# Five channel tiles of an up projection by seven products of summed quarters

## The chip, the cores and the metric

The kernel runs on one core of one Trainium2 chip. The metric is the time of one execution in device microseconds (us); a lower number is better. TensorE (PE) multiplies, VectorE (DVE), ScalarE (ACT) and GpSimd (POOL) do the elementwise work, and SyncE (SP) issues most of the loads.

## What is computed

The reference is one decoder layer over 512 positions and 1024 channels. The change lies in its last part, the gated MLP:

```python
h = rmsnorm(x, norm_ffn_pre[l])
u = causal_depthwise_conv(h @ w_ffn_up[l], ffn_conv_w[l], ffn_conv_b[l])
u_gate, u_val = jnp.split(u, 2, axis=-1)
y = (jax.nn.gelu(u_gate, approximate=True) * u_val) @ w_ffn_down[l]
x = x + rmsnorm(y, norm_ffn_post[l])
```

`h` is 512 x 1024 and `w_ffn_up` is 1024 x 5632: 2816 gate channels and 2816 value channels. The convolution looks back over two positions in each channel. Everything is float32.

## The kernel before

A float32 product is made of three matmuls in the format fp32r: each operand is split into a high part (an ACT copy that rounds) and a low part (a DVE subtraction, both in `split`, L81 to L88), and `mm3` (L127 to L130) adds high by high, high by low and low by high.

The up projection works channel-major. One channel tile is 128 gate channels and the 128 value channels that belong to them; there are 22 tiles, `f` from 0 to 21. Product `i = 2f` is the gate half of tile `f` and `i = 2f + 1` the value half. Each product has the weights as the stationary operand (128 x 128 blocks, eight of them over the 1024 input channels) and the normalized input `h1h`, `h1l` (high and low, transposed, both in tiles named hT) as the moving one, 512 positions at a time: 8 x 3 = 24 matmuls of 512 columns into one PSUM bank (`up_products`, L792 to L803). The first four products (`EARLY`) run in two halves of 256 columns (L764 and L802), because the second half of the input comes later.

The weights of a product are one 512 KB load into a `raw` buffer (four of them), issued on SP by `issue` (L95 to L117), and a split into a `whi` and a `wlo` buffer (three of each). `unit(b_up[i])` issues two products ahead.

The bank of a product goes through `conv` (L805 to L811): an ACT pass with the last tap and the bias, and two DVE passes that add the other two taps from the bank. The gate half takes a GELU on ACT (L822). The loop (L813 to L833) then multiplies the two halves on POOL into `gpair` (L829), and behind every fourth tile of the first twenty POOL makes four sums for the down projection (`sums`, L783 to L790). That projection already runs as seven products of summed quarters per 512 hidden channels.

PE runs in the order of the program, and POOL does so from L850 on. ACT and DVE are ordered by the planner at build time: among the instructions that are ready in its own model of time, the one that stands first in the program. On the chip each engine then goes through its list in that fixed order.

Of the kernel before, what the change touches and what calls it, by code (L numbers as in the profile page):

```python
# [26 lines left out]
NF = FH // P  # L27
# [11 lines left out]
def tile_hybrid_layer(  # L39
# [8 lines left out]
    act, dve, pool, pe, sp = nc.scalar, nc.vector, nc.gpsimd, nc.tensor, nc.sync  # L48
# [5 lines left out]
    wp = ctx.enter_context(tc.tile_pool(name="wp", bufs=3))  # L54
    mp = ctx.enter_context(tc.tile_pool(name="mp", bufs=2))
# [4 lines left out]
    ap = ap_stack.enter_context(tc.tile_pool(name="ap", bufs=2))  # L60
# [627 lines left out]
    h1l = T(mp, [P, KD, SEQ], F32R, "hT", 2)  # L688
    h1h = T(mp, [P, KD, SEQ], F32R, "hT", 2)
# [47 lines left out]
    banks = [[PT(tg) for tg in tags] for tags in ("ss", "tt")]  # L737
# [33 lines left out]
    fp = ctx.enter_context(tc.tile_pool(name="fp", bufs=2))  # L771
    c_tile = lambda: T(fp, [P, 512], F32, "c", 4)
    c_next = [c_tile()]
    gpair = [T(fp, [P, 4, 2, 256], F32, "G", NG) for _ in range(NG)]
    gsum = [[t[:, i, :] for i in range(3)] for t in (T(fp, [P, 3, 512], F32, "S", NG - 1) for _ in range(NG - 1))]
    gsum.append([T(mp, [P, 512], F32, "o", 3)[:] for _ in range(3)])
    grest = T(fp, [P, NF - NS, SEQ], F32, "gN", 1)

    def quarters(d):

        return [[gpair[d][:, 2 * c + r].rearrange("p j c -> p (j c)") for r in range(2)] for c in range(2)]

    def sums(d):  # L783

        (a11, a12), (a21, a22) = quarters(d)
        s1, s2, s4 = gsum[d]
        pool.tensor_tensor(s1, a21, a22, op=ALU.subtract)
        pool.tensor_tensor(s2, s1, a11, op=ALU.subtract)
        pool.tensor_tensor(a21, a11, a21, op=ALU.subtract)
        pool.tensor_tensor(s4, a12, s2, op=ALU.add)  # L790

    def up_products(i):  # L792

        if i in early:
# [18 lines left out]
    for f in range(NF):  # L813
# [7 lines left out]
        cg = conv(2 * f, banks[0])  # L821
        act.activation(cg[:], cg[:], AF.Gelu_apprx_tanh)  # L822
        if f:
            banks.append(list(up_products(2 * f + 1))[-1])
            issue(b_up[min(2 * f + 3, 2 * NF - 1)])
        cv = conv(2 * f + 1, banks[1])
        if f < NS:
            halves2 = lambda ap: ap.rearrange("p (c n) -> p c n", c=2)
            pool.tensor_tensor(gpair[f // 4][:, f % 2 :: 2, f % 4 // 2, :], halves2(cg[:]), halves2(cv[:]), op=ALU.mult)  # L829
        else:  # L830
            pool.tensor_tensor(grest[:, f - NS, :], cg[:], cv[:], op=ALU.mult)
        if f < NS and f % 4 == 3:
            sums(f // 4)  # L833
# [16 lines left out]
    ctx.enter_context(tc.manual_schedule(engines={mybir.EngineType.Pool}))  # L850
# [28 lines left out]
    def prepare(i):  # L879
# [76 lines left out]
    for i, (n, d) in enumerate(seq):  # L956
# [78 lines left out]
```

## Time and profile before

| | us |
|---|---|
| median of three runs | 828.42 (828.24 to 828.62) |
| the profiled execution | 828.08 |
| its span | 826.0 |
| PE busy | 812.1 |
| DVE busy | 496.5 |
| ACT busy | 399.3 |
| POOL busy | 138.5 |

The profiled execution is 2.08 us longer than its span. The granted clock of TensorE over the span is 0.997 of full speed. Busy times of PE overlap from one matmul to the next, so a pitch (start to start) is read for a matmul and not its duration.

### The profile page before, as it was taken

What the parts mean: (1) busy time and instruction counts of PE and PEld (TensorE: products, weight loads), DVE (VectorE), ACT (ScalarE), POOL (GpSimd) and SP (SyncE); (2) the same over time, 40 slices, a digit from 0 to 9 for tenths busy, and PEclk for the clock granted to TensorE, in tenths of its full rate; (3) what the DMA queues carried; (4) which work ended last, traced back from release to release, by engine and by line L of the source; (5) the groups of instructions that cost most, each with busy time, mean ns of one, the idle gap of its engine ahead of it and who ended that gap; (6) DMA issues with size and microseconds to landing.
All of it is one profiled execution on the core that took longest, in us unless ns stands there. A gap on an engine that the chain in (4) does not pass through costs nothing.

```text
span 826.0 us, 10558 instructions
## 1 busy us (share of the span) xinstructions
PE 812.1 (98%) x3955; PEld 683.8 (83%) x3955; DVE 496.5 (60%) x825; ACT 399.3 (48%) x693; POOL 138.5 (17%) x117
## 2 busy tenths in 40 slices
PE   6999999999999999999999999999999999999996
PEld 6888888888888888888888898888888888888885
DVE  5846576667667665634564555444554445678775
ACT  6735555556656655432352444343343333567552
POOL 5000000000001010112213101414131413442301
PEclk9999999999999999999999999999999999999998
DMA  9732223323332233324354203333333333696922
GB/s 298 232 94 79 74 84 90 87 85 103 88 92 78 82 102 90 101 85 127 115 183 137 77 27 112 92 102 102 101 87 93 102 102 102 153 222 162 223 83 102
DMA packets 123121, 93.99 MB, mean 114 GB/s; under 512 B 3543, under 2 KB 107167, under 8 KB 123071
## 3 DMA queue, kind: packets, MB, share of 16 engines
q1 hardware_dynamic: 116287, 79.16, 32.1%
q0 software_dynamic: 6160, 13.11, 8.1%
q10 hardware_dynamic: 624, 1.06, 0.3%
q8 instruction: 31, 0.51, 0.2%
q14 instruction: 19, 0.16, 0.1%
HBM read 91.18 MB, written 2.14 MB: 113 GB/s over the span
## 4 chain that ended last, share of the span: by engine, by line
PE 96%; DMA 2%; SPq 1%; issue 1%; DVE 0%; ACT 0%; DVEq 0%; POOLq 0%; POOL 0%
PE pj L128 22%; PE pj L129 22%; PE pj L130 22%; PE t L461 2%; PE s L486 2%; PE s L923 2%; PE s L922 2%; PE s L924 2%; PE t L923 1%; PE t L922 1%; PE t L924 1%; PE o L470 1%; PE o L469 1%; PE o L923 1%; PE o L922 1%; PE o L924 1%
## 5 line engine op out<-in xcount | busy, mean ns | idle before, releaser
L128 PE MATMUL pj<-hT,whi 128*128 128x512 f32 (+1 forms) x704 | 273.8, 389 | 0.0
L129 PE MATMUL pj<-hT,whi 128*128 128x512 f32 (+1 forms) x704 | 271.0, 385 | 0.0
L130 PE MATMUL pj<-hT,wlo 128*128 128x512 f32 (+1 forms) x704 | 271.0, 385 | 0.0
L85 DVE TENSOR_TENSOR wlo<-raw,whi 128x1024 fp32r<-128x1024 f32 x127 | 164.2, 1294 | 176.4 <-ACT whi L84 176.3
L84 ACT ACTIVATE whi<-raw 128x1024 fp32r<-128x1024 f32 x131 | 138.5, 1058 | 172.5 <-PE pj L129 131.4
L130 PEld LDWEIGHTS pj<-hT,wlo 128*128 128x128 f32 x704 | 132.3, 188 | 26.5
L128 PEld LDWEIGHTS pj<-hT,whi 128*128 128x128 f32 x704 | 132.4, 188 | 24.5
L129 PEld LDWEIGHTS pj<-hT,whi 128*128 128x128 f32 x704 | 132.5, 188 | 24.2
L602 POOL TENSOR_TENSOR mx<-mx,gt 128x512 f32<-128x512 f32 x16 | 23.0, 1436 | 379.2 <-DVE gt L601 379.2
L829 POOL TENSOR_TENSOR G<-c,c 128x512 f32<-128x512 f32 x20 | 25.8, 1288 | 167.2 <-DVE c L810 149.4
L128 PE MATMUL pj<-oT,whi 128*128 128x512 f32 (+1 forms) x128 | 48.1, 376 | 0.0
L129 PE MATMUL pj<-oT,whi 128*128 128x512 f32 (+1 forms) x128 | 47.0, 367 | 0.0
L130 PE MATMUL pj<-oT,wlo 128*128 128x512 f32 (+1 forms) x128 | 46.9, 367 | 0.0
L84 ACT ACTIVATE pt<-t 128x512 fp32r<-128x512 f32 (+2 forms) x48 | 24.3, 543 | 36.9 <-PE t L461 36.8
L85 DVE TENSOR_TENSOR pt<-t,pt 128x512 fp32r<-128x512 f32 (+2 forms) x48 | 28.5, 621 | 20.0 <-ACT pt L84 19.5
L488 ACT ACTIVATE P<-P,tiny 128x256 f32<-128x256 f32 (+1 forms) x64 | 33.0, 517 | 14.0 <-DVE tiny L487 13.8
L822 ACT ACTIVATE c<-c 128x512 f32<-128x512 f32 x22 | 13.9, 632 | 42.9 <-DVE c L810 42.9
L810 DVE SCALAR_TENSOR_TENSOR c<-pj,convw,c 128x510 f32<-128x510 f32 x40 | 30.0, 750 | 1.4
L808 ACT ACTIVATE c<-pj,convw 128x512 f32<-128x512 f32 x40 | 30.4, 760 | 0.0
L809 DVE SCALAR_TENSOR_TENSOR c<-pj,convw,c 128x511 f32<-128x511 f32 x40 | 29.7, 743 | 0.0
L130 PEld LDWEIGHTS pj<-oT,wlo 128*128 128x128 f32 x128 | 24.6, 192 | 3.8
L128 PEld LDWEIGHTS pj<-oT,whi 128*128 128x128 f32 x128 | 24.6, 192 | 3.3
(346 smaller groups left out, 1284.6 us busy)
## 6 DMA issues: line engine op xcount, KB each, us to landing
raw<-in_w_in_dram SPq DMA_DIRECT2D x46, 512.0 KB, 3.9
raw<-in_w_ffn_up_dram SPq DMA_DIRECT2D x44, 512.0 KB, 3.9
hT<-in_w_ffn_down_dram POOLq DMA_DIRECT2D x13, 512.0 KB, 8.3
raw<-in_w_ffn_down_dram POOLq DMA_DIRECT2D x12, 512.0 KB, 8.2
raw<-in_w_mem_kv_dram SPq DMA_DIRECT2D x8, 512.0 KB, 5.9
raw<-in_w_out_dram SPq DMA_DIRECT2D x8, 512.0 KB, 3.3
raw<-in_w_ffn_down_dram SPq DMA_DIRECT2D x8, 512.0 KB, 3.4
mx<-in_x_dram SPq DMA_DIRECT2D x12, 256.0 KB, 4.9
```

The source lines that it names most:

```text
L84: act.activation(hi, src, AF.Copy)
L85: eng.tensor_tensor(lo, src, hi.bitcast(F32), op=ALU.subtract)
L128: pe.matmul(ps, wh, xh, start=start, stop=False)
L129: pe.matmul(ps, wh, xl, start=False, stop=False)
L130: pe.matmul(ps, wl, xh, start=False, stop=stop)
L488: act.activation(dst, dst, AF.Exp, bias=mn[:, i : i + 1], scale=-1.0, accum_out=sm[:, i : i + 1])
L808: act.activation(c[:], ps[:], AF.Identity, scale=convw[:, 88 + ch : 89 + ch], bias=convw[:, 132 + ch : 133 + ch])
L809: dve.scalar_tensor_tensor(c[:, 1:512], ps[:, 0:511], convw[:, 44 + ch : 45 + ch], c[:, 1:512], op0=ALU.mult, op1=ALU.add)
L810: dve.scalar_tensor_tensor(c[:, 2:512], ps[:, 0:510], convw[:, ch : ch + 1], c[:, 2:512], op0=ALU.mult, op1=ALU.add)
L922: pe.matmul(ps[:], xh, wh, start=st, stop=False, skip_group_check=True)
L923: pe.matmul(ps[:], xh, wl, start=False, stop=False, skip_group_check=True)
L924: pe.matmul(ps[:], xl, wh, start=False, stop=end, skip_group_check=True)
```

## The change

Tiles 6, 8, 10, 12 and 14 (`SUP`) are computed in another way; tiles 7, 9, 11, 13 and 15 are computed as before, but their matmuls are interleaved with those of the tile ahead of them (`tile_pair`). All other tiles keep the loop.

For a tile in `SUP` the weights [gate | value] and the input are cut into quarters: input channels 0 to 511 and 512 to 1023, gate and value, positions 0 to 255 and 256 to 511. Seven products (`seventh`) of 4 x 3 = 12 matmuls of 256 columns each, of sums of weight quarters with sums of input quarters, replace the 48 matmuls of 512 columns. Three banks collect them; partial results are copied to SBUF or combined there (`p1_`, `u2_`, `p5_`, `row_g`, `row_v`), and `conv` reads the rows of SBUF in place of a bank.

Per tile in `SUP`, DVE makes four sums of weight quarters (`weight_sums`, 128 x 512 each), and there are splits of two whole weight tiles, of one half tile, and of the summed gate weights (`late`). The sums of the input are made once, by `input_sums`: eight POOL instructions over 128 x 1024 elements and eight splits of 128 x 512, one step of it behind each of tiles 0 to 4. They and `late` lie in buffers that tiles 0 to 15 don't need yet: four of the five `gpair` buffers, one of the `gsum` buffers, and buffers of the down projection. The order of POOL is that of the program from ahead of the loop on.

```diff
+SUP = (6, 8, 10, 12, 14)
...
     for i in range(2, 2 * NF):
-        up_block(i)
+        if i // 2 not in SUP:
+            up_block(i)
...
-    gpair = [T(fp, [P, 4, 2, 256], F32, "G", NG) for _ in range(NG)]
...
+    big_tile = lambda dt=F32: T(fp, [P, 2048], dt, "G", NG)[:]
...
+    parts = [big_tile().rearrange("p (a k c) -> p a k c", a=2, k=4) for _ in range(3)]
+    late = big_tile(F32R)
...
+        def whole(q, dst):
+            k, c = quarter_in[q]
+            pool.tensor_tensor(dst, h1h[:, k, c].bitcast(F32), h1l[:, k, c].bitcast(F32), op=ALU.add)
...
+        whole(3, a21)
+        yield
+        whole(4, a22)
+        pool.tensor_tensor(s1, a21, a22, op=ALU.subtract)
+        parted(1, s1)
+        yield
+        whole(1, a11)
+        pool.tensor_tensor(s2, s1, a11, op=ALU.subtract)
+        parted(2, s2)
+        yield
+        pool.tensor_tensor(a11, a11, a21, op=ALU.subtract)
+        parted(3, a11)
+        yield
+        whole(2, a12)
+        pool.tensor_tensor(a12, a12, s2, op=ALU.add)
+        parted(4, a12)
...
+    def weight_sums(raws):
+
+        (g0, g1), (v0, v1) = ((r[:, 0:512], r[:, 512:1024]) for r in raws)
+        first = wpair()
+        split(*first, raws[0])
+        split(*b22[0], v1)
+        for dst, other in ((g0, v0), (v0, v1), (v1, g0), (g1, v1)):
+            dve.tensor_tensor(dst, dst, other, op=ALU.add)
+        return first
...
+    def tile_pair(f, raws, first):
...
+        w_v = wpair()
+        split(*w_v, raws[1])
+        split(late_h, late_l, raws[0])
+        by, bx = PT("t"), PT("s")
+        seventh(by, first, 0, quarter_of(0, 0), True)
+        act.activation(p1_, by[:, 0:256], AF.Copy)
+        seventh(bx, first, 1, quarter_of(4, 0), True)
+        dve.tensor_tensor(row_g[:, 0:256], bx[:, 0:256], p1_, op=ALU.add)
+        steps(ng, 4)
+        seventh(by, w_v, 1, sum_of(2), False)
+        act.activation(u2_, by[:, 0:256], AF.Copy)
+        issue(b_up[2 * f + 3])
+        bz = PT("s")
+        seventh(bz, (late_h, late_l), 0, sum_of(1), True)
+        act.activation(p5_, bz[:, 0:256], AF.Copy)
+        cg_n = gate(2 * f + 2, steps(ng, 4))
+        raws = fetch_up(f + 2) if more else None
+        seventh(by, w_v, 0, sum_of(3), False)
+        dve.tensor_tensor(row_v[:, 256:512], p5_, by[:, 0:256], op=ALU.subtract)
+        first = weight_sums(raws) if more else None
+        issue(b_up[2 * f + (6 if more else 4)])
+        steps(nv, 4)
+        seventh(bz, w_22, 0, sum_of(4), False)
+        dve.tensor_tensor(row_v[:, 0:256], bz[:, 0:256], u2_, op=ALU.subtract)
+        cv = conv(2 * f + 1, row_v)
+        seventh(by, (late_h, late_l), 1, quarter_of(4, 256), False)
+        act.activation(row_g[:, 256:512], by[:, 0:256], AF.Copy)
+        gated(f, gate(2 * f, row_g), cv)
+        gated(f + 1, cg_n, conv(2 * f + 3, steps(nv, 4)))
+        return raws, first
+
+    ctx.enter_context(tc.manual_schedule(engines={mybir.EngineType.Pool}))
...
+        gated(f, cg, conv(2 * f + 1, banks[1]))
+        if f < SUP[0]:
+            next(making)
```

## Rows read from the trace of the kernel before

**Rows 1.** Parts 1 and 4 of the page: the busy time of each engine with its share of the span and its instructions, and the shares of the chain that ended last.

```profile
PE 812.1 (98%) x3955; PEld 683.8 (83%) x3955; DVE 496.5 (60%) x825; ACT 399.3 (48%) x693; POOL 138.5 (17%) x117
...
PE 96%; DMA 2%; SPq 1%; issue 1%; DVE 0%; ACT 0%; DVEq 0%; POOLq 0%; POOL 0%
```

**Rows 2.** Stretches of 20 us of the up projection: length, then busy time of PE, PEld, DVE, ACT and POOL with the instructions, the granted clock, the DMA share and GB/s; the last line sums ten such stretches.

```profile
545.00:565.00 20.00, 20.00 (x90) 16.57 (x89) 11.15 (x13) 8.12 (x11) 1.63 (x2) 1.00 0.30 89
...
sum 200.00, PE 200.00 PEld 169.03 DVE 100.16 ACT 77.19 POOL 46.58; mean PE 20.00 PEld 16.90 DVE 10.02 ACT 7.72 POOL 4.66
```

**Rows 3.** PE in order of time where the loop goes over from halves of 256 columns to products of 512 columns: start, duration, engine, line, operation, out<-in, shape.

```profile
495.35 0.28 PE L130 MATMUL pj<-hT,wlo 128*128 128x256 f32 x1
495.47 0.40 PE L128 MATMUL t<-hT,whi 128*128 128x512 f32 x1
...
496.86 0.39 PE L128 MATMUL t<-hT,whi 128*128 128x512 f32 x1
```

**Rows 4.** ACT, DVE and POOL in order of time over two products of the loop; the bracket is the idle time of the engine before the instruction and what ended it.

```profile
544.43 1.06 ACT L84 ACTIVATE whi<-raw 128x1024 fp32r<-128x1024 f32 x1 [3.71 <-PE pj L129]
545.39 0.76 ACT L808 ACTIVATE c<-pj,convw 128x512 f32<-128x512 f32 x1
545.52 1.23 DVE L85 TENSOR_TENSOR wlo<-raw,whi 128x1024 fp32r<-128x1024 f32 x1 [2.77 <-ACT whi L84]
546.66 0.74 DVE L809 SCALAR_TENSOR_TENSOR c<-pj,convw,c 128x511 f32<-128x511 f32 x1
...
549.87 1.06 ACT L84 ACTIVATE whi<-raw 128x1024 fp32r<-128x1024 f32 x1 [0.95 <-PE pj L129]
...
555.31 1.06 ACT L84 ACTIVATE whi<-raw 128x1024 fp32r<-128x1024 f32 x1 [3.71 <-PE pj L129]
```

**Rows 5.** PE in order of time in the early halves: the first and the last of 25 matmuls of 256 columns in a row.

```profile
476.45 0.28 PE L128 MATMUL pj<-hT,whi 128*128 128x256 f32 x1
...
479.33 0.28 PE L128 MATMUL pj<-hT,whi 128*128 128x256 f32 x1
```

**Rows 6.** PE in order of time at the end of six matmuls of 256 columns that stand between matmuls of 512.

```profile
70.53 0.28 PE L557 MATMUL s<-r,r 128*128 128x256 f32 x1
...
71.25 0.40 PE L128 MATMUL pj<-hT,whi 128*128 128x512 f32 x1
...
72.64 0.39 PE L128 MATMUL pj<-hT,whi 128*128 128x512 f32 x1
```

**Rows 7.** DVE's groups by form from 505 to 685 us: busy time, mean ns of one, idle time before.

```profile
L85 DVE TENSOR_TENSOR wlo<-raw,whi 128x1024 fp32r<-128x1024 f32 x33 | 40.5, 1226 | 89.6 <-ACT whi L84 89.6
L810 DVE SCALAR_TENSOR_TENSOR c<-pj,convw,c 128x510 f32<-128x510 f32 x32 | 24.0, 750 | 1.1
L809 DVE SCALAR_TENSOR_TENSOR c<-pj,convw,c 128x511 f32<-128x511 f32 x32 | 23.8, 743 | 0.0
L85 DVE TENSOR_TENSOR xl<-G,xh 128x512 fp32r<-128x512 f32 x3 | 2.1, 684 | 0.0
```

**Rows 8.** ACT's groups by form from 470 to 685 us, columns as above.

```profile
L84 ACT ACTIVATE whi<-raw 128x1024 fp32r<-128x1024 f32 x36 | 38.2, 1061 | 77.4 <-PE pj L129 72.8 <-PE t L129 3.3 <-issue 1.3
L808 ACT ACTIVATE c<-pj,convw 128x512 f32<-128x512 f32 x34 | 25.8, 760 | 0.0
L822 ACT ACTIVATE c<-c 128x512 f32<-128x512 f32 x19 | 12.0, 632 | 36.5 <-DVE c L810 36.5
L87 ACT ACTIVATE hT<-t,gam 128x256 fp32r<-128x256 f32 x5 | 2.4, 475 | 6.8 <-PE t L266 6.7
L84 ACT ACTIVATE xh<-G 128x512 fp32r<-128x512 f32 x3 | 1.8, 613 | 0.0
```

**Rows 9.** All instructions of L85, the low half of a split: count, then shortest, median and longest duration in ns, first and last start.

```profile
L85 DVE TENSOR_TENSOR r<-s,r x10: 416/424/425, 86.2 to 324.8; 128x256 fp32r<-128x256 f32 x10
...
L85 POOL TENSOR_TENSOR wlo<-raw,whi x4: 2347/2387/2412, 5.5 to 460.0; 128x1024 fp32r<-128x1024 f32 x4
```

**Rows 10.** POOL in order of time from the product of tile 3 on.

```profile
521.14 1.29 POOL L829 TENSOR_TENSOR G<-c,c 128x512 f32<-128x512 f32 x1 [9.59 <-DVE c L810]
522.50 1.29 POOL L787 TENSOR_TENSOR S<-G 128x512 f32<-128x512 f32 x1
523.88 2.26 POOL L788 TENSOR_TENSOR S<-S,G 128x512 f32<-128x512 f32 x1
526.09 1.30 POOL L789 TENSOR_TENSOR G<-G 128x512 f32<-128x512 f32 x1
527.35 1.29 POOL L790 TENSOR_TENSOR S<-G,S 128x512 f32<-128x512 f32 x1
532.01 1.29 POOL L829 TENSOR_TENSOR G<-c,c 128x512 f32<-128x512 f32 x1 [3.37 <-DVE c L810]
542.90 1.28 POOL L829 TENSOR_TENSOR G<-c,c 128x512 f32<-128x512 f32 x1 [9.60 <-DVE c L810]
```

**Rows 11.** DVE in order of time beside the third of these POOL instructions.

```profile
523.76 1.23 DVE L85 TENSOR_TENSOR wlo<-raw,whi 128x1024 fp32r<-128x1024 f32 x1 [2.77 <-ACT whi L84]
```

**Rows 12.** DVE in order of time near 717 us.

```profile
717.40 2.25 DVE L85 TENSOR_TENSOR wlo<-raw,whi 128x1024 fp32r<-128x1024 f32 x1
```

**Rows 13.** POOL in order of time at the same place.

```profile
716.99 1.59 POOL L831 TENSOR_TENSOR gN<-c,c 128x512 f32<-128x512 f32 x1
```

**Rows 14.** Part 6 of the page, the loads of the up weights: line, engine, operation, count, KB each, median us from issue to landing.

```profile
raw<-in_w_ffn_up_dram SPq DMA_DIRECT2D x44, 512.0 KB, 3.9
```

More of the change, by code (lines that the diff above doesn't have):

```diff
@@ new lines, in tile_hybrid_layer, with input_sums, parted @@
+    late = big_tile(F32R)
+    late_h, late_l = late[:, 0:1024], late[:, 1024:2048]
+    rows_s = T(fp, [P, 3, 512], F32, "S", NG - 1)
+    row_g, row_v = rows_s[:, 0, :], rows_s[:, 1, :]
+    p1_, u2_ = rows_s[:, 2, 0:256], rows_s[:, 2, 256:512]
+    p5_ = T(fp, [P, 512], F32, "gffn", 2)[:, 0:256]
+    b22 = T(fp, [P, 1024], F32R, "gN", 1)
+    b22 = [(b22[:, 0:512], b22[:, 512:1024])]
+    hsum = {}
+    def input_sums():
+        low, high = slice(0, 256), slice(256, 512)
+        quarter_in = {1: (slice(0, 4), low), 2: (slice(4, 8), low), 3: (slice(0, 4), high), 4: (slice(4, 8), high)}
+        a11, a21 = parts[0][:, 0], parts[0][:, 1]
+        a12, a22 = parts[1][:, 0], parts[1][:, 1]
+        s1, s2 = parts[2][:, 0], parts[2][:, 1]
+        def whole(q, dst):
+            k, c = quarter_in[q]
+            pool.tensor_tensor(dst, h1h[:, k, c].bitcast(F32), h1l[:, k, c].bitcast(F32), op=ALU.add)
+        def parted(j, src):
+            hsum[j] = []
+            for q in range(2):
+                hi, lo = (homes.pop(0).rearrange("p (k c) -> p k c", k=2) for _ in range(2))
+                split(hi, lo, src[:, 2 * q : 2 * q + 2, :])
+                hsum[j].append((hi, lo))
+        homes = [T(fp, [P, 512], F32R, tag, 3)[:] for tag in ("xh", "xl") for _ in range(3)]
+        homes += [T(mp, [P, 512], F32R, tag, n)[:] for tag, n in (("op", 2), ("gt", 2), ("o", 3)) for _ in range(n)]
+        for _ in range(2):
+            t = T(mp, [P, 1280], F32R, "P", 2)
+            homes += [t[:, 0:512], t[:, 512:1024]]
+        whole(3, a21)
[14 more added lines that the diff above has]
+        parted(4, a12)
+        b22.append((homes.pop(0), T(fp, [P, 512], F32R, "gffn", 2)[:]))
+        yield
+        yield
@@ L797, in up_products @@
         else:
-            u = unit(b_up[i])
-            ps = PT("t" if i < EARLY + 2 else "pj")
+            if i < 2 * SUP[0]:
+                issue(min(b_up[i] + 2, b_up[2 * SUP[0] - 1]))
+            u = units[b_up[i]] if i < 2 * max(SUP) + 4 else unit(b_up[i])
+            ps = PT("t" if i < EARLY + 2 else "s" if i < EARLY + 4 else "pj")
             a = 0
@@ L805, in conv @@
     def conv(i, ps):
+        ps = ps[:]
         ch = i // 2 + NF * (i % 2)
@@ L811, in conv, with gated @@
         return c
-    for f in range(NF):
+    def gated(f, cg, cv):
+        if f < NS:
+            if f % 4 == 0:
+                gpair[f // 4] = T(fp, [P, 4, 2, 256], F32, "G", NG)
+            halves2 = lambda ap: ap.rearrange("p (c n) -> p c n", c=2)
+            pool.tensor_tensor(gpair[f // 4][:, f % 2 :: 2, f % 4 // 2, :], halves2(cg[:]), halves2(cv[:]), op=ALU.mult)
+        else:
+            pool.tensor_tensor(grest[:, f - NS, :], cg[:], cv[:], op=ALU.mult)
+        if f < NS and f % 4 == 3:
+            d = f // 4
+            if d < NG - 1:
+                t = T(fp, [P, 3, 512], F32, "S", NG - 1)
+                gsum[d] = [t[:, i, :] for i in range(3)]
+            else:
+                gsum[d] = [T(mp, [P, 512], F32, "o", 3)[:] for _ in range(3)]
+            sums(d)
@@ new lines, in gate, with steps, fetch_up @@
+    def gate(i, bank):
+        cg = conv(i, bank)
+        act.activation(cg[:], cg[:], AF.Gelu_apprx_tanh)
+        return cg
+    def steps(gen, n):
+        for _ in range(n):
+            ps = next(gen)
+        return ps
+    def fetch_up(f):
+        raws = []
+        for c in (f, NF + f):
+            raw = T(wp, [P, 1024], F32, "raw", 4)[:]
+            sp.dma_start(raw.rearrange("p (k c) -> p k c", k=KD), w_ffn_up[0][:, c * P : (c + 1) * P].rearrange("(k p) c -> p k c", p=P))
+            raws.append(raw)
+        return raws
@@ new lines, in wpair, with seventh @@
+    def wpair():
+        return T(wp, [P, 1024], F32R, "whi", 3)[:], T(wp, [P, 1024], F32R, "wlo", 3)[:]
+    def weight_sums(raws):
[6 more added lines that the diff above has]
+        return first
+    def seventh(ps, w, half, x, st):
+        wh, wl = (a[:, half * 512 : half * 512 + 512] for a in w)
+        for k in range(4):
+            c = slice(k * P, (k + 1) * P)
+            xh, xl = x(k)
+            pe.matmul(ps[:, 0:256], wh[:, c], xh, start=st and k == 0, stop=False, skip_group_check=True)
+            pe.matmul(ps[:, 0:256], wh[:, c], xl, start=False, stop=False, skip_group_check=True)
+            pe.matmul(ps[:, 0:256], wl[:, c], xh, start=False, stop=k == 3, skip_group_check=True)
@@ new lines, in quarter_of, with sum_of @@
+    def quarter_of(k0, c0):
+        return lambda k: (h1h[:, k0 + k, c0 : c0 + 256], h1l[:, k0 + k, c0 : c0 + 256])
+    def sum_of(j):
+        return lambda k: tuple(a[:, k % 2, :] for a in hsum[j][k // 2])
+    def tile_pair(f, raws, first):
+        more = f + 2 in SUP
+        w_22 = b22[0]
+        b22.reverse()
+        ng, nv = up_products(2 * f + 2), up_products(2 * f + 3)
+        w_v = wpair()
[28 more added lines that the diff above has]
+        return raws, first
@@ L814, in tile_hybrid_layer @@
+    ctx.enter_context(tc.manual_schedule(engines={mybir.EngineType.Pool}))
+    making = input_sums()
+    f = 0
+    while f < NF:
+        if f in SUP:
+            raws, first = tile_pair(f, raws, first)
+            f += 2
+            continue
         if f == 0:
@@ L820, in tile_hybrid_layer @@
             banks = [list(up_products(2 * f))[-1]]
-        cg = conv(2 * f, banks[0])
-        act.activation(cg[:], cg[:], AF.Gelu_apprx_tanh)
+        cg = gate(2 * f, banks[0])
         if f:
             banks.append(list(up_products(2 * f + 1))[-1])
[L825 to L833, printed above, removed]
+            if f + 1 in SUP:
+                raws = fetch_up(f + 1)
+                first = weight_sums(raws)
+                issue(b_up[2 * f + 4])
+            else:
+                issue(b_up[min(2 * f + 3, 2 * NF - 1)])
+        gated(f, cg, conv(2 * f + 1, banks[1]))
+        if f < SUP[0]:
+            next(making)
+        if f + 1 == NS:
+            grest = T(fp, [P, NF - NS, SEQ], F32, "gN", 1)
+        f += 1
     gffn = [T(fp, [P, 512], F32, "gffn", 2) for _ in range(2)]
```

5 lines of the change are left out of this document (1 added, 4 removed).

## The prediction

> **What bounds the kernel now.** I read the busy shares and the chain that ended last first: PE is busy for 98% of the span and is 96% of the chain [rows 1]. Then the stretches of the up projection: PE is busy for 200.00 of 200 us at full clock, while DVE is at 100.16, ACT at 77.19 and POOL at 46.58 [rows 2]. So this stage takes as long as its matmuls take, and the other engines have half their time to spare. A change is worth what it takes from PE, less what PE then waits.
>
> **Matmul time.** A plain product starts every 5.44 us: the weight splits that PE's release of a buffer starts stand at 544.43, 549.87 and 555.31 [rows 4]. That is 5.44 / 24 = 0.2267 us per matmul of 512 columns, and 2 x 5.44 = 10.88 us per tile. Of 256 columns, 24 pitches take 479.33 - 476.45 = 2.88 us, 0.1200 each [rows 5]. That is more than half of 0.2267, so the smaller matmuls give part of the saving back. A tile in seven products costs 7 x 12 x 0.1200 = 10.08 us in place of 10.88. The change takes out 0.80 us per tile, 4.0 us in five. I take the pitch of the early halves because the form is the same: 128 x 128 weights, three matmuls per block, 256 moving columns.
>
> In the trace columns alone don't set the pitch (0.1200 against 0.1133, half of 0.2267). The Trainium skill, TensorE: Matmul & The Clock Gate, section Back-to-back issue gap, gives N / 2.4 + 2.5 ns, 109 and 216 ns. By that a tile would go from 10.36 to 9.17 us, an estimate of 5.9 us saved in five. The rows are 0.011 us longer at either size and decide here.
>
> A return from 256 to 512 columns costs a little. Six matmuls of 512 behind the switch take 72.64 - 71.25 = 1.39 us [rows 6] and 496.86 - 495.47 = 1.39 [rows 3], against 6 x 0.2267 = 1.36. That is 0.03 us, four times per pair (ahead of each half of the plain products), 0.12 x 5 = 0.6 us. **Matmuls: -4.0 + 0.6 = -3.4 us.** All of it lies on the path, since PE is never idle there.
>
> **Per pair, in steady state.** A pair (one new tile, one plain) has 10.08 + 10.88 + 0.12 = 21.1 us of PE. Counted from its first matmul, PE does: two sevenths to 2.9; half the plain gate to 5.6; two sevenths to 8.5; the other half to 11.2; one to 12.7; half the plain value to 15.4; two to 18.3; the rest to 21.1. The work beside it, by [rows 7 to 9]:
> - DVE: five low halves of 1.23, one of 0.68, four weight sums of 0.68 (same form as xl<-G), three row operations of 0.42, eight convolution passes of 0.75: 6.1 + 0.7 + 2.7 + 1.3 + 6.0 = 16.8 us of 21.1, 80%, against 10.9 for two plain tiles.
> - ACT: five high halves of 1.06, one of 0.61, four 256-wide copies at 0.47, four convolutions of 0.76, two GELUs of 0.63: 5.3 + 0.6 + 1.9 + 3.0 + 1.3 = 12.1 us, 57%.
>
> Both fit, but the DVE work comes late. The weight buffer of `first` for the next pair comes free with the plain gate at 11.2, that of `w_v` with the plain value at 21.1, and the third seventh needs the low half of `w_v` at 21.1 + 5.6 = 26.7. From the first bank's ACT pass (12.2) to there DVE has four convolutions (6.0), two row operations (0.8), `first` (1.23), the half tile (0.68), four sums (2.7), the next plain gate (1.23) and `w_v` (1.23): 13.9 us, in a window of 14.4. Successive DVE instructions overlap by 0.09 us (545.52 + 1.23 against 546.66 [rows 4]), some 15 x 0.09 = 1.3 us; the slack is 1.8 us. Inside that window stand POOL products of 1.29 us, which can hold DVE up (below). So the stall is 0 to about 1 us per pair, 0 to 5 us in all. I take 0.1 per pair, 0.5 us, because one POOL instruction fits into the slack and a late pair lengthens the window of the next.
>
> The copies of a bank that PE adds to again (`p1_`, `u2_`, `row_v`) are due 3.8 us or more behind their seventh, and cost 0.47 or 0.42: hidden while ACT and DVE are on time. The loads are as many and as big as before. `fetch_up` on SP waits for the split of `late`, near 6 us of a pair, and the load of the next plain gate is queued behind it; at 3.9 us to landing [rows 14] the raws are there near 10 to 12, when `first` can start. Were that late, it would add to the DVE window; I take 0.
>
> **Entry: the input sums.** On POOL, steps 0 to 4 add eight instructions of 128 x 1024 at 2.39 us [rows 9], 19.1 us over six tiles. The nearest row is the same two-input form, so I take it as it stands. Eight splits of 0.61 on ACT and 0.68 on DVE go with them. All but the last steps are hidden: the first are due 40 us later. The last ones are not free. POOL's four down-projection sums end at 527.35 + 1.29 = 528.6 [rows 10]. Then: the third difference (2.39) to 531.0; its two splits to about 533.1; the product of tile 4, which now waits for them because its buffer holds that difference (1.29), to 534.5; two instructions of 2.39 to 539.4. Queued behind the new wait on POOL are these two and tile 5's product; for them wait the fourth sum's splits, and whatever stands behind those on ACT and DVE. The first pair starts when product 12 did, 495.47 [rows 3] + 8 x 5.44 = 539.0. The fourth sum itself is needed only by the sixth seventh, 15.4 us into the pair, at 554.4.
>
> POOL and DVE also disturb each other. The POOL sum that began 0.12 us behind a DVE low half took 2.26 us against 1.29 for its neighbours, and the DVE one stayed at 1.23 [rows 10, 11]; the other way round, a low half that began 0.41 us into a POOL product took 2.25 [rows 12, 13]. Both have two inputs in SBUF. So they exclude each other, the one that began first going on. The Trainium skill, GPSIMD Engine Reference, section Specifications, states a contention on shared SBUF interfaces with DVE instructions that have two SBUF inputs; the trace agrees. Between 529 and 540 DVE has about 8.5 us of such work (two plain low halves and `first` at 1.23, the half tile at 0.68, four weight sums and two splits of the third difference at 0.68), so the fourth sum ends between 539.4 and about 548. What that costs depends on the planned order: nothing if its splits stand behind `p1_` and `w_v`; if they stand ahead, those wait for POOL, and the third seventh, due at 539.0 + 5.6 = 544.6, starts as late as 548 + 1.2 + 1.2 = 550.4. Bounds 0 to 6 us. I take 0.5, near the lower end: POOL's last instruction ends by its own rows behind 539.0, when the high half of `w_v` is already ready, so the planner has reason to put that first.
>
> **Sum.** -4.0 + 0.6 + 0.5 + 0.5 = -2.4 us. The profiled execution would go from 828.08 to 825.7 (span 823.6); its median stands 0.34 higher, at 828.42, so I forecast 826.0.
>
> **Rivals.**
> 1. *DVE becomes the bound in each pair.* If the window is overrun by 0.4 to 0.7 us each time, 2 to 3.4 us go: 827.0 to 828.4. For it: 80% busy, POOL inside the window. Against: each stall also gives DVE time. Chance 0.17.
> 2. *The entry stalls; slower.* The fourth sum's splits stand ahead of `p1_` or `w_v` on ACT or DVE and POOL is late by contention. Place: the third seventh of the first pair, once. It decides from a stall of 5.1 us (it must pay 3.4 and then 1.7); at 6 us the time is 828.4 - 3.4 + 6 = 831.0. For it: the sum chain ends 0.4 us behind the pair's start even undisturbed, and the planner may not see the exclusion. Against: its use is 10 us later than that of `w_v`. Chance 0.24 for slower, and 0.08 for a stall of 2 to 5 us, which is within the noise.
> 3. *The change doesn't do what it says.* The new matmuls run at more than 10.88 / 84 = 0.1295 us, because they change banks every 12. The early halves, which change every 24, show nothing of it. 828.4; chance 0.03.
> 4. *All hidden:* no stalls, 825.0, down to 824.4 without the switch cost. Chance 0.05.
>
> **How the numbers follow.** The forecast (825.3 to 826.7) has 0.43. A difference under 0.2% (1.7 us) is about what a measurement of this kernel can't tell from none. Faster: 0.43 + 0.05 = 0.48. Within: 0.17 + 0.08 + 0.03 = 0.28. Slower: 0.24. The range goes from just under the all-hidden case, 824.6, to rival 2 at its bound, 831.0; the likeliest case alone has 825.3 to 826.7.
>
> **What the profile will show.** PE's pitch at 0.120 in the sevenths and 0.227 in the plain halves; 420 matmuls of 256 columns where 240 of 512 stood; about 3.4 us between the products' times with no idle PE. The stretch from the start of product 12 to that of product 32 is 108.8 us now (20 x 5.44) and should be about 106. A gap in PE ahead of the third seventh of the first pair, released by an ACT or DVE instruction behind a split of the summed input, speaks for rival 2; a gap at the same place in each pair, behind `wlo` on DVE, for rival 1. I am wrong if either adds up to more than 2 us, or if tiles 0 to 5 lose time to POOL.

## The result, and the profile after

The changed kernel takes 834.57 us (median of 6 runs, 834.25 to 835.09), the kernel before 828.52 (828.19 to 829.07) beside it: ratio 1.0071, 95% interval [1.0061, 1.0081]. It is 6.05 us slower; the forecast was 826.0 with a range up to 831.0. The profiled execution has a span of 832.2 us against 826.0.

The page of the changed kernel: busy time of each engine, the chain that ended last, and POOL's product of the two halves of a tile (L879).

```profile
PE 811.2 (97%) x4135; PEld 690.2 (83%) x4135; DVE 534.8 (64%) x878; ACT 417.2 (50%) x731; POOL 164.8 (20%) x125
...
PE 85%; DMA 4%; DVE 3%; POOL 3%; issue 2%; ACT 1%; SPq 1%; POOLq 0%; DVEq 0%; ACTq 0%
...
L879 POOL TENSOR_TENSOR G<-c,c 128x512 f32<-128x512 f32 x20 | 31.4, 1571 | 144.3 <-ACT c L893 86.4
```

PE's share of the chain fell from 96% [rows 1] to 85%; DVE and POOL, 0% before, are in it now with 3% each. POOL's product takes 1571 ns in the mean against 1.29 us [rows 10], although it is the same instruction.

Stretches of the changed kernel, columns as in [rows 2]: four of 20 us, 2.9 us out of the third, and the three pairs from the second to the fourth:

```profile
505.00:525.00 20.00, 20.00 (x90) 16.57 (x89) 12.75 (x16) 10.89 (x15) 10.58 (x5) 1.00 0.34 99
525.00:545.00 20.00, 17.62 (x90) 14.88 (x88) 14.81 (x14) 5.26 (x8) 18.23 (x9) 1.00 0.11 33
545.00:565.00 20.00, 16.50 (x90) 14.57 (x91) 14.33 (x20) 9.85 (x15) 1.29 (x1) 0.83 0.36 106
565.00:585.00 20.00, 20.00 (x126) 18.04 (x125) 14.55 (x20) 10.34 (x16) 8.82 (x6) 1.00 0.37 106
...
545.60:548.50 2.90, 0.00 (x0) 0.03 (x1) 2.90 (x5) 2.90 (x6) 0.00 (x0) 0.50 0.43 123
...
568.56:631.68 63.12, 63.12 (x397) 57.23 (x396) 49.15 (x64) 32.33 (x49) 21.35 (x14) 1.00 0.36 102
```

PE is idle in two neighbouring stretches only. In the first of them POOL is busy for 18.23 of 20 us; in the second the granted clock is 0.83 in the mean, and it is at 0.50 while PE still stands idle. PE itself, in order of time:

```profile
542.34 0.28 PE L931 MATMUL s<-hT,wlo 128*128 128x256 f32 x1
548.50 0.76 PE L129 MATMUL pj<-hT,whi 128*128 128x512 f32 x1 [5.88 <-DVE c L870]
549.06 0.63 PE L130 MATMUL pj<-hT,whi 128*128 128x512 f32 x1
549.49 0.63 PE L131 MATMUL pj<-hT,wlo 128*128 128x512 f32 x1
...
552.44 0.40 PE L129 MATMUL pj<-hT,whi 128*128 128x512 f32 x1
552.68 0.40 PE L130 MATMUL pj<-hT,whi 128*128 128x512 f32 x1
...
568.56 0.28 PE L929 MATMUL t<-hT,whi 128*128 128x256 f32 x1
...
631.68 0.28 PE L929 MATMUL t<-hT,whi 128*128 128x256 f32 x1
```

Two sevenths of the first pair are done when PE waits 5.88 us for a bank: the plain gate (product 14) needs the one that DVE's second convolution pass (L870) of product 10 still reads. Behind the wait the engine is at 1.2 GHz for nine matmuls of 512 columns: the second starts 0.56 us behind the first, and the eight steps from there to 552.44, most of them 0.43 us instead of 0.2267, take 3.38 us in place of 1.81, another 1.6 us. The last two lines are the starts of the second and the fifth pair: (631.68 - 568.56) / 3 = 21.04 us per pair, with no idle PE.

Why that bank is late, in order of time on POOL, ACT and DVE (L826, L802 and L830 are the third difference, the last quarter and the fourth sum; L86 is the low half of a split, L920 a weight sum):

```profile
533.93 2.84 POOL L826 TENSOR_TENSOR G<-G 128x1024 f32<-128x1024 f32 x1
536.73 1.29 POOL L879 TENSOR_TENSOR G<-c,c 128x512 f32<-128x512 f32 x1
537.99 2.84 POOL L802 TENSOR_TENSOR G<-hT,hT 128x1024 f32<-128x1024 f32 x1
540.91 2.71 POOL L830 TENSOR_TENSOR G<-G,G 128x1024 f32<-128x1024 f32 x1
```

```profile
536.81 0.63 ACT L85 ACTIVATE gt<-G 128x512 fp32r<-128x512 f32 x1 [6.40 <-POOL G L826]
```

```profile
537.47 1.10 DVE L86 TENSOR_TENSOR gt<-G,gt 128x512 fp32r<-128x512 f32 x1 [2.95 <-ACT gt L85]
538.50 2.88 DVE L920 TENSOR_TENSOR raw<-raw,raw 128x512 f32<-128x512 f32 x1
541.31 2.86 DVE L86 TENSOR_TENSOR o<-G,o 128x512 fp32r<-128x512 f32 x1
544.09 0.68 DVE L920 TENSOR_TENSOR raw<-raw,raw 128x512 f32<-128x512 f32 x1
...
547.62 0.73 DVE L870 SCALAR_TENSOR_TENSOR c<-pj,convw,c 128x510 f32<-128x510 f32 x1
```

Two things stand in this stretch. ACT, in its fixed order, has stood 6.40 us at the split of the third difference, and DVE behind it 2.95. Then two DVE instructions of 0.68 us take 2.88 and 2.86, each ending some 0.5 us behind the POOL sum that it met. The pass L870 of product 10 is queued behind all of these.

**Ledger of the two profiled executions** (span 6.2 us longer). From the first matmul of product 4 to the first of the down projection 221.96 us against 217.62: +4.34. The wait, taken from start to start, is 6.37 of it: 6.16 - 0.12 = 6.04 from 542.34 to 548.50, and 0.33 in the slow first matmul behind it. The half clock is 1.57, so the matmuls gave back 3.6. The down projection 106.75 against 105.86: +0.9. The start of product 4 is 0.57 later (496.04 against 495.47 [rows 3]) and the tail 0.4 longer.

The down projection loses on POOL's queue. Its accumulating loads in the changed kernel and in the kernel before, in order of time:

```profile
721.89 1.60 POOL L881 TENSOR_TENSOR gN<-c,c 128x512 f32<-128x512 f32 x1 [9.60 <-DMA hT<-in_w_ffn_down_dram]
723.43 5.07 POOL L1034 DMA_DIRECT2D raw<-in_w_ffn_down_dram  x4
```

```profile
704.83 1.35 POOL L863 DMA_DIRECT2D raw<-in_w_ffn_down_dram  x1 [2.10 <-DVE wlo L85]
...
719.95 1.20 POOL L863 DMA_DIRECT2D raw<-in_w_ffn_down_dram  x1 [1.38 <-DVE wlo L85]
```

With POOL in the order of the program from ahead of the loop, all four stand behind the last product; before, the planner had put three of them ahead of it. The first of them is issued 723.43 - 704.83 = 18.6 us later, and the stage starts 4.9 us later (718.00 against 713.09): 13.7 us lost against its use.

### The profile page after: what moved, and what is told of

Same layout as the page of the kernel before. It is cut to its first block, busy times and chain, and to the rows that moved or that the text cites. A ratio compares the mean times of both kernels' runs of the same rounds, so it can differ in the third digit from the quotient of the medians.

```text
span 832.2 us, 10999 instructions
## 1 busy us (share of the span) xinstructions
PE 811.2 (97%) x4135; PEld 690.2 (83%) x4135; DVE 534.8 (64%) x878; ACT 417.2 (50%) x731; POOL 164.8 (20%) x125
## 4 chain that ended last, share of the span: by engine, by line
PE 85%; DMA 4%; DVE 3%; POOL 3%; issue 2%; ACT 1%; SPq 1%; POOLq 0%; DVEq 0%; ACTq 0%
PE pj L129 18%; PE pj L130 18%; PE pj L131 18%; DMA raw<-in_w_ffn_down_dram 2%; PE t L463 2%; PE s L488 2%; PE s L1094 1%; PE s L1095 1%; PE s L1093 1%; PE t L931 1%; PE t L930 1%; PE t L929 1%; PE o L472 1%; DVE wlo L86 1%; PE o L471 1%
## 5 line engine op out<-in xcount | busy, mean ns | idle before, releaser
L86 DVE TENSOR_TENSOR wlo<-raw,whi 128x1024 fp32r<-128x1024 f32 x127 | 166.8, 1314 | 130.7 <-ACT whi L85 130.6
L129 PE MATMUL pj<-hT,whi 128*128 128x512 f32 (+1 forms) x608 | 237.6, 391 | 5.9 <-DVE c L870 5.9
L130 PE MATMUL pj<-hT,whi 128*128 128x512 f32 (+1 forms) x608 | 234.6, 386 | 0.0
L131 PE MATMUL pj<-hT,wlo 128*128 128x512 f32 (+1 forms) x608 | 234.3, 385 | 0.0
L85 ACT ACTIVATE whi<-raw 128x1024 fp32r<-128x1024 f32 x131 | 138.5, 1057 | 135.8 <-PE pj L130 84.1
L129 PEld LDWEIGHTS pj<-hT,whi 128*128 128x128 f32 x608 | 115.0, 189 | 26.3 <-ACT whi L85 6.1
L131 PEld LDWEIGHTS pj<-hT,wlo 128*128 128x128 f32 x608 | 114.7, 189 | 23.2
L130 PEld LDWEIGHTS pj<-hT,whi 128*128 128x128 f32 x608 | 115.0, 189 | 19.8
L879 POOL TENSOR_TENSOR G<-c,c 128x512 f32<-128x512 f32 x20 | 31.4, 1571 | 144.3 <-ACT c L893 86.4
L85 ACT ACTIVATE pt<-t 128x512 fp32r<-128x512 f32 (+2 forms) x48 | 24.3, 543 | 36.9 <-PE t L463 36.8
L86 DVE TENSOR_TENSOR pt<-t,pt 128x512 fp32r<-128x512 f32 (+2 forms) x48 | 28.5, 620 | 20.0 <-ACT pt L85 19.5
L1094 PE MATMUL s<-wlo,xh 128*128 128x512 f32 x70 | 27.5, 392 | 0.1
L129 PEld LDWEIGHTS pj<-oT,whi 128*128 128x128 f32 x128 | 24.6, 192 | 3.3
L130 PEld LDWEIGHTS pj<-oT,whi 128*128 128x128 f32 x128 | 24.6, 192 | 3.3
L1095 PE MATMUL s<-whi,xl 128*128 128x512 f32 x70 | 27.2, 389 | 0.0
## 6 DMA issues: line engine op xcount, KB each, us to landing
raw<-in_w_ffn_down_dram POOLq DMA_DIRECT2D x12, 512.0 KB, 10.9
```

What stands on the lines that cost most here:

```text
L1094: pe.matmul(ps[:], xh, wl, start=False, stop=False, skip_group_check=True)
L1095: pe.matmul(ps[:], xl, wh, start=False, stop=end, skip_group_check=True)
```

## Experiments

Each ran beside the kernel before (828.33 to 828.74). The theories: the sums end too late, because POOL's third difference stands behind its four sums for the down projection (A; its part A2 is the stop of ACT and DVE behind that difference); POOL's sums over 128 x 1024 cost wherever they meet a busy DVE, by exclusion and by the stops of ACT and DVE behind them (D; its narrower form, exclusion beside the weight sums alone, is A1); the first pair has too much DVE work of its own (B); POOL's order costs the down projection its loads (C). "Wait" is what PE's starts in the up stage lose in pauses and in the slow matmul just behind each (6.37 us in the change, where the profile's own idle time is 5.88); "half clock" is what the matmuls at 1.2 GHz lose behind that (1.57 in the change). Where one ends and the other begins is worth some 0.3 us.

**defer_sums.** The first group's sums for the down projection go behind the last input sum.

```diff
-            sums(d)
+            if d:
+                sums(d)
...
+        if f == SUP[0] - 1:
+            sums(0)
```

> The four down-projection sums of the first tile group, which stood on POOL between the second and the third difference of the input (527.4 to 533.9 us in the changed kernel's profile), are put behind the last input sum. Theory A (POOL is late with the third difference; ACT and DVE stand still behind it in their fixed order, PE's bank isn't read, and PE waits 5.9 us and then runs 9 matmuls at half clock, 1.9 us): the third difference starts about 6.5 us earlier, the wait and the slow clock go, 834.6 - 7.8 = 826.8 us (825.8 to 828). Theory B (DVE and ACT have too much work ahead of the first pair, whoever makes the sums): 833 to 835.

834.67 us, 1.0073 [1.006, 1.0086]; wait 4.99, half clock 1.40. The third difference is done by 529.5, as meant, and nothing is won: the last two sums stand at 537.04 and 539.96, and beside them a weight sum takes 2.77 us and a low half 3.43. Lateness alone (A) falls.

**sums_on_dve.** All eight input sums go to DVE.

```diff
-            pool.tensor_tensor(dst, h1h[:, k, c].bitcast(F32), h1l[:, k, c].bitcast(F32), op=ALU.add)
+            dve.tensor_tensor(dst, h1h[:, k, c].bitcast(F32), h1l[:, k, c].bitcast(F32), op=ALU.add)
...
-        pool.tensor_tensor(a11, a11, a21, op=ALU.subtract)
+        dve.tensor_tensor(a11, a11, a21, op=ALU.subtract)
```

> The eight input sums of 128x1024 are made on DVE and not on POOL. Theory A (POOL's lateness and its exclusion with DVE): DVE does one in some 1.23 us, where POOL took 2.4 to 3.4, and nothing waits for POOL; no wait of PE at the entry, 826.8 us (825.8 to 828). Theory B (too much work on DVE ahead of the first pair): DVE gets 8 x 1.23 = 9.8 us more, the wait stays or grows, 834 to 840.

826.39 us, 0.9974 [0.9964, 0.9983]; wait 0. DVE has eight instructions more, seven of 1.21 us and one of 2.32 beside a POOL product, 10.8 us, and the wait is gone: it isn't the amount of DVE's work that was too much, nor the buffers in which the sums lie. The planner orders ACT and DVE in another way here; unused_on_pool, below, takes that out.

**start_at_8.** Tile 6 stays plain; the input sums are made where they were.

```diff
-SUP = (6, 8, 10, 12, 14)
+SUP = (8, 10, 12, 14)
...
-            next(making)
+            next(making, None)
```

> Tile 6 is plain, so four tiles in seven products (8, 10, 12, 14) in place of five, and two more tiles between the input sums and the first pair. Theory A (the input sums are late for the first pair): no wait at the entry, four pairs give 4 x 0.68 = 2.7 us, the later loads of the down projection cost about 1: 828.5 - 2.7 + 1 = 826.8, up to 827.5. Theory B (the work of any first pair): the wait moves to tile 8's pair, 834 to 836.

835.32 us, 1.0086 [1.0073, 1.01]; a wait of 5.17 us at 540.96, between plain tiles (6.06 in all, half clock 2.54). No pair is near: the first pair's own work (B) isn't the cause. The last two sums, at 538.09 and 541.02, meet two low halves here (2.89 and 3.35 us) and no weight sum.

**before_pool_order.** The kernel before, with POOL's order fixed from ahead of the loop, and nothing else.

```diff
+    ctx.enter_context(tc.manual_schedule(engines={mybir.EngineType.Pool}))
     for f in range(NF):
...
-    ctx.enter_context(tc.manual_schedule(engines={mybir.EngineType.Pool}))
```

> The kernel before, with the one change that POOL goes in the order of the program from ahead of the up projection on, and not from behind it. Theory C (in that order the accumulating loads of the down projection stand behind POOL's last product of the up projection, some 14 us later than before, and the first down products wait for them): 829.5 us, 1.0 slower, with the loads issued from 721 us on. Rival (these loads are covered, and the 1 us in the changed kernel's down projection has another cause): 828.5.

829.54 us, 1.0013 [1.0004, 1.0022]; the up stage is 217.62 as before, the down projection 107.10 against 105.86. The moved line costs 1.2 us by itself (0.3 to 1.8 by the interval). That it does so through the loads isn't tested apart; here too all four are issued behind POOL's last product, from 718.74 us on.

**last_on_dve, third_on_dve.** The last two sums, or the third difference alone, go to DVE.

```diff
-        whole(2, a12)
-        pool.tensor_tensor(a12, a12, s2, op=ALU.add)
+        dve.tensor_tensor(a12, h1h[:, 4:8, 0:256].bitcast(F32), h1l[:, 4:8, 0:256].bitcast(F32), op=ALU.add)
+        dve.tensor_tensor(a12, a12, s2, op=ALU.add)
```

```diff
-        pool.tensor_tensor(a11, a11, a21, op=ALU.subtract)
+        dve.tensor_tensor(a11, a11, a21, op=ALU.subtract)
```

> Of the eight input sums only the last two (step 4, 2.84 and 2.71 us on POOL beside DVE's weight sums) are made on DVE. Theory A1 (these two POOL instructions hold DVE's two-input instructions up when DVE has most to do): DVE does them in 2 x 1.23, the wait of PE goes or falls under 1 us, 826.5 to 828. Theory A2 (the third difference is late on POOL and the fixed order of ACT and DVE stops behind it): the wait stays above 3 us, 831 to 835.

> Only the third difference (step 3, behind the four down-projection sums on POOL) is made on DVE. Theory A1: the last two sums still run on POOL beside the weight sums, PE waits 3 us or more and runs at half clock after it, 831 to 835. Theory A2: nothing stops behind POOL's third difference, 826.5 to 828.

831.07 us (1.0027 [1.0016, 1.0039], wait 3.0, half clock 1.4) and 832.70 (1.0054 [1.0042, 1.0067], wait 4.7, half clock 1.56). Each takes away a part, the two late sums more than the one early one. With the third difference on DVE, a weight sum and a low half beside the last sums still take 2.76 and 3.42 us.

**dve_sums_old_pool.** As sums_on_dve, and POOL's order fixed where it was in the kernel before.

```diff
-    ctx.enter_context(tc.manual_schedule(engines={mybir.EngineType.Pool}))
     making = input_sums()
...
+    ctx.enter_context(tc.manual_schedule(engines={mybir.EngineType.Pool}))
     keep = [T(mp, [P, 1280], F32, "P", 2) for _ in range(2)]
```

> All input sums on DVE, and POOL goes in the order of the program only from the place where it did in the kernel before. Theory C (that order cost the down projection some 1.0 to 1.2 us): its accumulating loads start some 14 us earlier again, 826.4 - 1.1 = 825.3 (825.0 is the forecast's case with everything hidden). Rival (the 1 us comes from the up projection's ending later or from other buffers): 826.4.

825.25 us (825.06 to 825.86), 0.9959 [0.9945, 0.9973]: faster than both kernels. Up stage 214.26 (-3.36 against before), down projection 105.86, as before.

**step_ahead.** Each step of the sums goes ahead of its tile's product on POOL.

```diff
-        gated(f, cg, conv(2 * f + 1, banks[1]))
         if f < SUP[0]:
             next(making)
+        gated(f, cg, conv(2 * f + 1, banks[1]))
```

> Each step of the input sums stands ahead of its tile's product on POOL and not behind it, about one tile (11 us) earlier; all eight stay on POOL. Theory A1 and A2: the last two sums end ahead of the weight sums, no wait of PE at the first pair or one under 1.5 us, 826.5 to 829. Theory D (any 128x1024 sum on POOL costs DVE its length, wherever it stands, and DVE has no time to spare in tiles 0 to 5): 831 to 835.

832.75 us, 1.0052 [1.004, 1.0065]; wait 4.98. The last two sums still fall on 535 to 541, behind the sums for the down projection, and two weight sums in a row beside them take 5.57 us. Inconclusive on the order itself; it moved the meeting too little.

**last_late.** The last two sums, on POOL as in the change, one step later.

```diff
         parted(3, a11)
         yield
+        yield
         whole(2, a12)
...
         yield
-        yield
```

> The last two input sums stay on POOL but go one tile later, behind tile 5's product, when the weight sums of the first pair are done on DVE. Theory A1 (exclusion beside the weight sums): the plain gate of the first pair finds its bank read on time, the wait there goes; POOL's 5 us fall into the first pair instead, whose DVE slack I put at 1.8 us, so 1 to 3 us are lost there: 828 to 830. Theory A2 (what hurts is the stop behind the third difference): the wait ahead of the plain gate stays, 832 to 835.

828.38 us, 0.9995 [0.9986, 1.0004]: 6.2 us less than the change, with the same instructions on the same engines. The wait is 1.66, no matmul runs at half clock. PE, ACT and DVE of this run up to the plain gate of the first pair, in order of time:

```profile
543.83 0.47 PE L129 MATMUL pj<-hT,whi 128*128 128x512 f32 x1 [1.50 <-DVE c L870]
```

```profile
536.52 0.63 ACT L85 ACTIVATE gt<-G 128x512 fp32r<-128x512 f32 x1 [6.41 <-POOL G L826]
```

```profile
537.19 1.10 DVE L86 TENSOR_TENSOR gt<-G,gt 128x512 fp32r<-128x512 f32 x1 [2.95 <-ACT gt L85]
538.22 0.68 DVE L920 TENSOR_TENSOR raw<-raw,raw 128x512 f32<-128x512 f32 x1
538.82 0.68 DVE L86 TENSOR_TENSOR o<-G,o 128x512 fp32r<-128x512 f32 x1
...
542.95 0.73 DVE L870 SCALAR_TENSOR_TENSOR c<-pj,convw,c 128x510 f32<-128x510 f32 x1
```

This settles how the change's wait divides. Up to L870 of product 10, DVE goes through the same list as in the change, and PE has the same list throughout. ACT stands 6.41 us at the split of the third difference and DVE 2.95 behind it, as in the change (6.40 and 2.95). But the two instructions behind that, which took 2.88 and 2.86 us beside the last two sums, take 0.68 each, 4.38 less together, and PE's idle time is 1.50 us in place of 5.88, also 4.38 less. So 4.4 us of the change's wait are the exclusion by these two sums. The other 1.5 come with the stop behind the third difference and with smaller lengthenings ahead of it, and aren't divided further.

Where the two sums went, POOL and DVE, in order of time:

```profile
548.71 2.39 POOL L802 TENSOR_TENSOR G<-hT,hT 128x1024 f32<-128x1024 f32 x1
551.18 2.40 POOL L831 TENSOR_TENSOR G<-G,G 128x1024 f32<-128x1024 f32 x1
```

```profile
554.28 0.69 DVE L86 TENSOR_TENSOR P<-G,o 128x512 fp32r<-128x512 f32 x1 [6.68 <-ACT o L85]
```

The sums take 2.39 and 2.40 us, undisturbed: DVE is idle for the 6.68 us in which they run, and what then waits for them isn't due yet.

**after_old_pool.** The change, with POOL's order fixed where it was before; the planner then puts all the sums early.

The edit is the same as in dve_sums_old_pool, without that of sums_on_dve:

```diff
-    ctx.enter_context(tc.manual_schedule(engines={mybir.EngineType.Pool}))
     making = input_sums()
```

> The changed kernel, with only the place from which POOL goes in the order of the program put back to where it was. By its list, POOL then makes all eight input sums ahead of tile 3's product, and the down projection's loads start early again. Theory A1: nothing of the input sums stands beside the weight sums of tiles 4 and 5, so the wait at the first pair goes; with the loads' 1.1 us back, 825.3 to 827. Theory D (128x1024 sums on POOL cost DVE their length wherever they stand): the waits move to tiles 1 to 3, 830 to 834.

833.90 us, 1.0067 [1.0055, 1.008]; wait 6.80, half clock 1.60, now at 528.9, ahead of the pairs, behind four sums in a row from 498.72 (11.45 us). The down projection is back at 105.85. The sums meet DVE between 503 and 523 us (low halves of 2.54, 2.56, 2.34 and, last, 3.41 us), where it makes no weight sums, so "beside the weight sums alone" (A1) falls and D stands.

**six_tiles.** As dve_sums_old_pool, with six tiles.

```diff
-SUP = (6, 8, 10, 12, 14)
+SUP = (5, 7, 9, 11, 13, 15)
```

> All input sums on DVE, POOL's order as in the kernel before, and six tiles in seven products (5, 7, 9, 11, 13, 15). If the gain is 0.68 us per tile and DVE's work is done in time: 825.25 - 0.7 = 824.6. If DVE, which has one tile less to make the sums, is late for the first pair: one wait of 1 us or more, 825.5 to 828.

829.31 us (827.62 to 831.04), 1.001 [1.0001, 1.0019]: above both forecasts. PE is idle for 3.1 us, and some matmuls behind that run at half clock. The first pair comes 10.9 us earlier, and PE waits 2.7 us for the low half of `late`, which itself takes 2.28 us beside a POOL product. How much of this is DVE's lack of room for the sums, and how much that product, isn't shown.

**unused_on_pool.** As sums_on_dve, and beside each of the last five sums POOL makes a sum that nobody reads.

```diff
         whole(1, a11)
+        pool.tensor_tensor(a22, h1h[:, 0:4, 0:256].bitcast(F32), h1l[:, 0:4, 0:256].bitcast(F32), op=ALU.add)
...
```

> All input sums are on DVE, as in the run with them there (826.39 us, no wait of PE in the up stage), and POOL makes five more 128 x 1024 sums whose result nothing reads: one beside each of the last five input sums, in the same steps behind tiles 2 to 4. No instruction of ACT or DVE waits for them. If POOL's 128 x 1024 sums cost through the exclusion alone (DVE instructions that meet them grow by up to 2.2 us each), DVE falls behind although it waits for nothing: a wait of PE of 2 us or more comes back ahead of or in the first pair, and the time is 829 to 833. If they cost because ACT and DVE, in their fixed order, stop for their results, nothing comes back: 826.0 to 827.0, no wait of PE over 0.5 us, although DVE instructions beside them are still seen at 2 to 3.4 us. In between, both have a share.

837.17 us (834.98 to 838.5), 1.0095 [1.0081, 1.0109], 10.8 us more than without the five, and more than the 829 to 833 expected; the up stage is 225.83 against 214.28, with 8.14 us of wait and 3.6 of half clock. The orders of PE, ACT and DVE are the same, instruction for instruction, in both. DVE without them, then DVE, POOL and PE with them, in order of time:

```profile
520.25 0.68 DVE L86 TENSOR_TENSOR o<-G,o 128x512 fp32r<-128x512 f32 x1
520.85 0.68 DVE L86 TENSOR_TENSOR P<-G,o 128x512 fp32r<-128x512 f32 x1
...
537.70 1.22 DVE L86 TENSOR_TENSOR wlo<-raw,whi 128x1024 fp32r<-128x1024 f32 x1
```

```profile
520.04 2.88 DVE L86 TENSOR_TENSOR o<-G,o 128x512 fp32r<-128x512 f32 x1
522.84 2.88 DVE L86 TENSOR_TENSOR P<-G,o 128x512 fp32r<-128x512 f32 x1
...
543.92 3.43 DVE L86 TENSOR_TENSOR wlo<-raw,whi 128x1024 fp32r<-128x1024 f32 x1
547.27 0.74 DVE L874 SCALAR_TENSOR_TENSOR c<-pj,convw,c 128x511 f32<-128x511 f32 x1
```

```profile
519.53 2.84 POOL L823 TENSOR_TENSOR G<-hT,hT 128x1024 f32<-128x1024 f32 x1
522.44 2.73 POOL L825 TENSOR_TENSOR G<-hT,hT 128x1024 f32<-128x1024 f32 x1
...
546.35 3.23 POOL L835 TENSOR_TENSOR G<-hT,hT 128x1024 f32<-128x1024 f32 x1
```

```profile
532.76 0.47 PE L129 MATMUL pj<-hT,whi 128*128 128x512 f32 x1 [3.94 <-DVE c L875]
533.07 0.39 PE L130 MATMUL pj<-hT,whi 128*128 128x512 f32 x1
533.30 0.55 PE L131 MATMUL pj<-hT,wlo 128*128 128x512 f32 x1
533.64 0.63 PE L129 MATMUL pj<-hT,whi 128*128 128x512 f32 x1
534.07 0.63 PE L130 MATMUL pj<-hT,whi 128*128 128x512 f32 x1
```

Nothing waits for the five results, and from 515 to 555 us no instruction of ACT or DVE waits for POOL at all, so this is the exclusion alone: each sum holds one DVE instruction up, four of them by about 2.2 us (0.68 to 2.88, 1.22 to 3.43) and the last by 1.5. It is enough to stop PE twice; that the sums' results are waited for isn't needed.

## Why the prediction was wrong

| term | forecast | measured |
|---|---|---|
| matmuls and switches | -3.4 | -3.36 (up stage of dve_sums_old_pool) |
| stalls of the pairs | +0.5 | none (21.04 us per pair, 21.1 forecast) |
| entry: input sums on POOL | +0.5, bounds 0 to 6 | +7.9 (6.37 wait + 1.57 half clock) |
| POOL's order on the down projection | not costed | +1.2 (before_pool_order) |
| sum | -2.4 | +6.05 |

The four measured terms make +5.8. The rest, 0.25, is well inside the interval (5.1 to 6.7 us); the 0.57 us by which product 4 starts later in the profile differs from one profiled run to the next and stays unexplained.

**Right: the matmul terms.** The pitches of [rows 5] and [rows 4] and the switch of [rows 3, 6] carried over to the new form. Rival 3 is out. The all-hidden case, 825.0, is what dve_sums_old_pool gives: 825.25. The estimate of 5.9 us saved, by the Trainium skill, TensorE: Matmul & The Clock Gate, section Back-to-back issue gap, isn't borne out: the up stage became 3.36 us shorter. That section gives the formula for an isolated matmul, not for a stream of weight loads and matmuls as here.

**Right: the pairs.** DVE is busy for 49.15 / 3 = 16.4 us per pair (16.8 forecast), and PE never waits for it there: the slack held. (From 12.2 to 26.7 its window is 14.5 us, not 14.4.) Rival 1 is out.

**Failed: the entry term.** The step was "I take 0.5, near the lower end", with the whole cost laid on the fourth sum and its place put at the third seventh, "nothing if its splits stand behind `p1_` and `w_v`". I had the exclusion from [rows 10 to 13], and counted it as a delay of POOL's chain. That chain did end inside the bounds given, at 543.62 us (539.4 to 548), although it began late: the third difference ends at 536.77, not at 531.0, since the product of tile 3 starts at 525.15 and not at 521.14. The cost lay elsewhere. The runs show it as a delay of DVE's list: the instruction that each sum holds up has everything behind it in DVE's list, also the convolution that frees a bank for PE. So it struck at the plain gate's bank, behind two sevenths, not at the third seventh or the sixth. The slack that I gave it was that of the data's use (15 us); the one that counted was that of the next bank. Rival 2 had the right sign and the exclusion as its ground, but a wrong place, and at 6 us as a bound too small a price.

**Failed: its upper bound.** A wait of PE was priced as its length. In the change the wait is followed by nine matmuls at half clock, 1.6 us more. With 7.9 us in place of 6, and 1.2 for the loads, rival 2's sum is 828.4 - 3.4 + 7.9 + 1.2 = 834.1, against 834.57 measured.

**Left out: the moved POOL order.** I followed POOL's new order for the sums, and not for the loads that are queued there too. It costs 1.2 us on the kernel before (before_pool_order), and 1.1 between sums_on_dve and dve_sums_old_pool (1.5 when each is taken beside its own kernel before).

**What is shown and what isn't.** Shown: without POOL's sums no wait (sums_on_dve), with unused ones a wait (unused_on_pool), and with the last two sums in DVE's idle time 4.38 us less of it, as much as the two DVE instructions are shorter (last_late). Of the change's 5.88 us, 4.4 are therefore the exclusion beside the last two sums. Not settled is how the other 1.5 divide between the stop of ACT and DVE for the third difference and the lengthenings ahead of it.

The Trainium skill, SBUF — State Buffer, section Who interferes with whom, says that a DVE instruction with two SBUF inputs contends with a GpSimd instruction that reads SBUF, and that contention there is an exclusive lock. The trace agrees: 0.68 us became 2.88 beside a POOL sum, while a convolution pass, which reads a bank and one SBUF tile, stays at 0.74 beside one (547.27). The price here is about 2.2 us of DVE per 128 x 1024 sum. POOL pays too: the sum at 537.99 in the change takes 2.84 us, against 2.39 undisturbed, and at its start DVE's low half of 537.47 still runs, for 0.58 us more.

## What to carry to other kernels

Cost an instruction moved to POOL as time on DVE, not only on POOL: each two-input one that meets a busy DVE stops it for nearly its own length (here about 2.2 us beside a sum of 2.7 to 2.85), and what pays is whatever DVE's list has next for PE. In this kernel eight sums are 10.8 us of DVE work and, with five tiles, nothing on the path; on POOL, "free", they cost 8 us of the path. If such work must be on POOL, find the stretch in which DVE is idle (last_late), and when an order is fixed by hand, follow every DMA issued on that queue.

## What was not expected of the hardware

A POOL sum does not only hold up the DVE instruction that it meets: with sums in a row, one DVE instruction gets through per sum. Two low halves of 0.68 us took 2.88 each beside POOL's 2.84 and 2.73, and two weight sums in a row 5.57 in step_ahead.

The clock can fall in the wait or only behind it. In the change it is at 0.50 from 545.6 us on, while PE stands idle until 548.50. In unused_on_pool the first three matmuls behind 3.94 us of idle time start 0.31, 0.23 and 0.34 us apart, and only then every 0.43: there it was still at full speed when PE went on. Behind a wait of 1.66 us (last_late) it did not fall.
